# Three direct tiles in place of four per SwiGLU block, and the first round's additions to x by transfers from GpSimd

## The chip, the cores and the metric

The kernel runs on one core of one Trainium2 chip. The metric is the device time of one execution in microseconds (us); lower is better. The profile names the engines PE (TensorE, matmuls), PEld (its weight loads), DVE (VectorE), ACT (ScalarE), POOL (GpSimd) and SP (SyncE, which here issues transfers).

## The reference

One decoder layer of a Hymba/Conformer kind on 512 positions of width 1024, all in float32:

```python
x = x + 0.5 * swiglu(rms_norm(x, g_ffn1), w_ffn1_gate, w_ffn1_up, w_ffn1_down)
h = rms_norm(x, g_mix); proj = h @ w_in          # attention, conv and memory parts
...
x = x + concatenate([y_attn, y_conv, y_mem]) @ w_out
x = x + 0.5 * swiglu(rms_norm(x, g_ffn2), w_ffn2_gate, w_ffn2_up, w_ffn2_down)

def swiglu(x, w_gate, w_up, w_down):
    return (silu(x @ w_gate) * (x @ w_up)) @ w_down   # 1024 -> 2816 -> 1024
```

The change touches the two SwiGLU blocks alone; the mixing stage between them stays as it is.

## The kernel before

x lies in SBUF as eight tiles of 128 features by 512 positions (`x[:, d]`, d = 0 to 7). Every float32 product is made of three matmuls on split operands: each operand has a high part (`whi`, `xh`, `hh`, `bh`) and a low part (`wlo`, `xl`, `hl`, `bl`), and PE adds high by high, low by high and high by low in PSUM (`mm3`, L337 to L339).

**A SwiGLU block** (`ffn`) runs over 22 hidden tiles f of 128 features. The first `N_DIRECT` tiles are *direct*: gate and up take 24 matmuls of 512 columns each; `evac` (L403 to L410) scales the two products, applies the SiLU and multiplies, and `hidden` (L395 to L398) splits the result into `hh` (ACT) and `hl` (DVE). The remaining tiles are *fast* (`fast`): a scheme with fewer multiplications on two-by-two blocks makes gate and up out of seven half-size products (`product`, L439 to L441), 84 matmuls of 256 columns. It needs sums of blocks of x, which `blocks(k)` makes for k = 0 to 3 while the direct tiles run (`braw` and `bmade` on DVE, L427 to L429, their high parts `bh` on ACT, L426 and L430, their low parts `bl` on DVE, L431 and L432), and sums of the weights, `s12` and `s43`, which `make_sums` makes on DVE for each tile (L124 to L127). A few products pass through ACT (L450, L454, L456: PSUM to `kept`).

**Weights** (`Weights`) are loaded on SP's queue into four raw buffers (`wraw`), 512 KB at most each; ACT casts the high part (L165) and DVE subtracts for the low one (L166) into four slots used in turn. A slot is free when PE has read its last. In a name such as `wlo12` the number counts the weight pieces in order.

**The downs.** The hidden tiles are taken in rounds (`ROUNDS`). When a round is complete, `down(r, g)` multiplies its tiles with their part of the third weight, for each of the eight d, and DVE adds half the result to `x[:, d]` (L496). A load carries the weights of `8 // (tiles of the round)` of the d (`per_load`). `steps(f)` sets where they stand: the downs of a round lie among the tiles of the next one; those of the first round, all but the last load, stand ahead of the next round's first tile, which is the first fast one.

The order on each engine is fixed when the kernel is built, by a scheduler that moves instructions within what data and buffers allow; each engine then works its own list in order and waits at semaphores. Small work tiles `t` (`work()`) share five buffers in turn; PSUM has four banks for `mm`, two for `sc`, two for `tp`.

Of the kernel before, what the change touches and what calls it, by code (L numbers as in the profile page):

```python
# [34 lines left out]
AF = mybir.ActivationFunctionType  # L35
ALU = mybir.AluOpType
# [35 lines left out]
TILES = [s[1:] for s in ORDER if s[0] == "p"]  # L72

ON_DVE = [(0,), (1, 3), (1, 3), (2, 3), (1, 3), (1, 3)]
ROUNDS = [(0, 4), (4, 8), (8, 12), (12, 16), (16, 18), (18, 22)]
N_DIRECT = 4
N_ACT = 20

SUM_BUFS = 3
# [4 lines left out]
class Weights:  # L84
# [95 lines left out]
    def next(self):  # L180
        i = self.at
        self.at += 1
        self.split_to(i + 1 + self.conv_ahead)
        return self.split.pop(i)


def per_load(r):

    return 8 // (ROUNDS[r][1] - ROUNDS[r][0])


def steps(f):

    r = next(r for r, (lo, hi) in enumerate(ROUNDS) if lo <= f < hi)
    if r == 0:
        return [], [], []
    i, n, m = f - ROUNDS[r][0], ROUNDS[r][1] - ROUNDS[r][0], KT // per_load(r - 1)
    if r == 1:
        return [(r - 1, g) for g in range(m - 1)] if i == 0 else [], [(r - 1, m - 1)] if i == 1 else [], []
    mine = [(r - 1, g) for g in range(i * m // n, (i + 1) * m // n)]  # L200
    return [], mine[:1], mine[1:]


def layer(tc, ctx, a):
    nc = tc.nc
    PE, ACT, DVE, POOL = nc.tensor, nc.scalar, nc.vector, nc.gpsimd
# [8 lines left out]
    def nm(s):  # L215
        uid[0] += 1
        return f"{s}_{uid[0]}"

    def mm_bank():
        return psum.tile([P, T], F32, tag="mm", name=nm("mm"), bufs=4)  # L220

    def sc_bank():
        return psum.tile([P, T], F32, tag="sc", name=nm("sc"), bufs=2)
# [4 lines left out]
    def work():  # L228
        return tmp.tile([P, T], F32, tag="t", name=nm("t"), bufs=5)
# [7 lines left out]
    def flat(w):  # L237
        return w.rearrange("p k m -> p (k m)")

    def ffn_weights(n, memory):  # L240
        gu = a[f"wgu{n}"]

        def down(r, g):
            lo, hi = ROUNDS[r]
            m = per_load(r)
            return a[f"wd{n}"][g * m : (g + 1) * m, :, lo:hi].rearrange("d p k m -> p d (k m)")

        for f in range(NF):
            pre, mid, post = steps(f)
            for d in pre:  # L250
                W.add(down(*d), 128)
            if f < N_DIRECT:
                W.add(flat(gu[f, 0]))
# [5 lines left out]
            if memory and f == MEM_F:  # L259
                for t in range(2):  # L260
                    W.add(flat(a["wmk"][t]))
                for c in range(2):
                    W.add(flat(a["wmv"][:, 4 * c : 4 * c + 4]))
        r = len(ROUNDS) - 1
        for g in range(KT // per_load(r)):
# [21 lines left out]
    def atile(name, dtype=F32R):  # L287
        return act.tile([P, T], dtype, tag="h", name=nm(name), bufs=N_ACT)
# [45 lines left out]
    def mm3(ps, wh, wl, ks, hi, lo, first, last, woff=0):  # L334
        for i, k in enumerate(ks):
            w = slice((k - woff) * P, (k - woff + 1) * P)
            PE.matmul(ps, wh[:, w], hi(k), start=first and i == 0, stop=False)  # L337
            PE.matmul(ps, wh[:, w], lo(k), start=False, stop=False)  # L338
            PE.matmul(ps, wl[:, w], hi(k), start=False, stop=last and i == len(ks) - 1)  # L339
# [4 lines left out]
    def scaled_split(d, gcol):  # L344

        g = par[:, gcol + d : gcol + d + 1]
        xh[d], xl[d] = atile("xh"), atile("xl")
        ACT.activation(xh[d], x[:, d], AF.Identity, scale=g)
        DVE.scalar_tensor_tensor(xl[d], x[:, d], g, xh[d].bitcast(F32), op0=ALU.mult, op1=ALU.subtract)  # L349
# [39 lines left out]
    def ffn(pool, norm, first, gain, hooks, next_gain, last):  # L389
# [5 lines left out]
        def hidden(f, t):  # L395
            h_hi[f], h_lo[f] = atile("hh"), atile("hl")
            ACT.copy(h_hi[f], t)
            DVE.tensor_tensor(h_lo[f], t, h_hi[f].bitcast(F32), op=ALU.subtract)  # L398
# [13 lines left out]
        def blocks(k):  # L412

            raw = pool.tile([P, 4, 256], F32, tag="sum", name=nm("braw"), bufs=SUM_BUFS)
            made = pool.tile([P, 4, 256], F32, tag="sum", name=nm("bmade"), bufs=SUM_BUFS)
            flat_raw = raw.rearrange("p a b -> p (a b)")
            for i, d in enumerate((k + 4, k)):
                DVE.scalar_tensor_tensor(
                    flat_raw[:, i * T : (i + 1) * T], x[:, d], par[:, gain + d : gain + d + 1], rb, op0=ALU.mult, op1=ALU.mult
                )  # L420
            b21, b22, b11, b12 = (raw[:, i] for i in range(4))
            bh[k] = pool.tile([P, 7, 256], F32R, tag="bh", name=nm("bh"), bufs=4)
            bl[k] = pool.tile([P, 7, 256], F32R, tag="bl", name=nm("bl"), bufs=4)
            if k == 0:
                pool.tile([P, 16], F32, name=nm("shift"))
            ACT.copy(bh[k][:, 4:7], raw[:, 0:3])  # L426
            DVE.tensor_tensor(made[:, B_T3 : B_Q1 + 1], raw[:, 1:3], raw[:, 3:4].to_broadcast([P, 2, 256]), op=ALU.subtract)  # L427
            DVE.scalar_tensor_tensor(made[:, B_Q2], made[:, B_T3], -1.0, b11, op0=ALU.mult, op1=ALU.subtract)
            DVE.tensor_tensor(made[:, B_T4], b21, made[:, B_Q2], op=ALU.add)  # L429
            ACT.copy(bh[k][:, 0:4], made)  # L430
            DVE.tensor_tensor(bl[k][:, 4:7], raw[:, 0:3], bh[k][:, 4:7].bitcast(F32), op=ALU.subtract)  # L431
            DVE.tensor_tensor(bl[k][:, 0:4], made, bh[k][:, 0:4].bitcast(F32), op=ALU.subtract)  # L432
# [46 lines left out]
        def down(r, g):  # L479

            lo, hi = ROUNDS[r]
            end = r == len(ROUNDS) - 1
            wh, wl = W.next()

            def step(j):
                d = g * per_load(r) + j
                cut = last and end and d == KT - 1
                for t0, t1 in [(0, T // 2), (T // 2, T)] if cut else [(0, T)]:
                    ps = mm_bank()[:, : t1 - t0]
                    mm3(  # L490
                        ps, wh, wl, range(lo, hi), lambda k: h_hi[k][:, t0:t1], lambda k: h_lo[k][:, t0:t1],
                        True, True, woff=lo - j * (hi - lo),
                    )
                    xd = x[:, d, t0:t1]
                    o = work()[:, : t1 - t0] if last and end else xd
                    DVE.scalar_tensor_tensor(o, ps, 0.5, xd, op0=ALU.mult, op1=ALU.add)  # L496
                    if last and end:
                        nc.sync.dma_start(a["out"][d, :, t0:t1], o)
                if end and not last:
                    nxt.add(d)  # L500
                    scaled_split(d, next_gain)

            return [lambda j=j: step(j) for j in range(per_load(r))]
# [3 lines left out]
        raw = {}  # L507
        for f in range(NF):
            pre, mid, post = steps(f)
            for d in pre:  # L510
                for step in down(*d):
                    step()
            if f >= N_DIRECT:
                fast(f, mid)
            else:
                g, u = (sc_bank(), sc_bank()) if f % 3 == 2 else (mm_bank(), mm_bank())
                gh, gl = W.next()
                if f == 0:
                    uh, ul = W.next()
                    for ks in first:  # L520
                        mm3(g, gh, gl, ks, xhk, xlk, ks[0] == 0, ks[-1] == 7)
                        mm3(u, uh, ul, ks, xhk, xlk, ks[0] == 0, ks[-1] == 7)
                    norm.stats()
                    held = (g, u)
                else:
                    mm3(g, gh, gl, range(8), xhk, xlk, True, True)
                    if f == 1:
                        norm.spread()
                        raw[0] = evac(0, *held)
                        blocks(0)  # L530
                        hidden(0, raw[0])
                    uh, ul = W.next()
                    mm3(u, uh, ul, range(8), xhk, xlk, True, True)
                    raw[f] = evac(f, g, u)
                    if f == 1:
                        hidden(1, raw[1])
                    blocks(f)
                if f == N_DIRECT - 1:
                    for i in range(2, N_DIRECT):
                        hidden(i, raw[i])  # L540
            for d in post:
                for step in down(*d):
                    step()
            for hook in hooks.get(f, ()):
                hook()
        r = len(ROUNDS) - 1
# [168 lines left out]
    with tc.tile_pool(name="fast1", bufs=1) as pool:  # L715
        norm = ffn(pool, norm, STARTS, C_G1, hooks, C_GM, False)
# [4 lines left out]
    with tc.tile_pool(name="fast2", bufs=1) as pool:  # L721
        ffn(pool, norm, [[0, 1, 2, 3, 4, 5, 6], [7]], C_G2, {}, None, True)
# [484 lines left out]
```

## Time and profile before

| | |
|---|---|
| runs | 883.81, 884.22, 884.62 us; median 884.22 |
| the profiled execution | 884.99 us, span 883.2 us |
| first block: direct tile 4, downs of round 0, first fast tile | start at 48.01, 59.00, 75.80 us |
| second block: the same | start at 573.59, 584.58, 601.38 us |

The span is the time from the first to the last instruction that the profiler recorded; times in the trace count from its start. The profiled execution is one more run beside the three. The lines themselves are shown with the prediction.

### The profile page before, as it was taken

The page shows a single profiled execution, that of the slowest core. Times are in us where ns is not written, and L with a number is a line of the kernel's source. Part 1 is how long each engine was busy: PE and PEld are TensorE (multiplying, and loading weights), DVE is VectorE, ACT ScalarE, POOL GpSimd, SP SyncE. Part 2 cuts the span into 40 slices and gives each one's busy share as a digit, 9 for nine tenths or more (in the row PEclk, how much of TensorE's full clock was granted, in tenths as well). Part 3 has the DMA queues.
Part 4 walks back from the last instruction along what each step waited for, and adds up shares of the span by engine and source line. Part 5 has one row for each costly group of instructions (what it writes and reads, how often), then busy time and mean ns, then how long its engine had stood idle before and what let it go on. Part 6 is the DMA issues. An engine that isn't in the chain of part 4 may idle for free.

```text
span 883.2 us, 13993 instructions
## 1 busy us (share of the span) xinstructions
PE 869.9 (98%) x5522; PEld 760.4 (86%) x5525; DVE 713.1 (81%) x1121; ACT 438.2 (50%) x733; POOL 45.9 (5%) x38
## 2 busy tenths in 40 slices
PE   7999999999999999999999999999999999999998
PEld 3889999899999999888666788889999999989997
DVE  7999978986796886769999776999987878777872
ACT  6454554454563445533929754345554444534540
POOL 6000000000020000300020021000000000000000
PEclk9999999999999999999999999999999999999999
DMA  5522333333334244231010232323334332332312
GB/s 196 167 96 86 106 120 108 109 108 119 119 121 129 87 120 144 72 101 60 4 57 13 84 100 92 96 72 124 104 107 120 96 118 85 111 117 72 120 48 96
DMA packets 34082, 88.45 MB, mean 100 GB/s; under 512 B 3168, under 2 KB 7008, under 8 KB 34016
## 3 DMA queue, kind: packets, MB, share of 16 engines
q1 hardware_dynamic: 32864, 85.99, 30.9%
q10 hardware_dynamic: 1152, 1.57, 0.6%
q8 instruction: 43, 0.70, 0.3%
q14 instruction: 23, 0.19, 0.1%
HBM read 85.45 MB, written 2.10 MB: 99 GB/s over the span
## 4 chain that ended last, share of the span: by engine, by line
PE 93%; DVE 4%; DMA 1%; issue 1%; ACT 0%; SPq 0%; DVEq 0%
PE mm L337 15%; PE mm L339 15%; PE mm L338 15%; PE mm L439 11%; PE mm L441 11%; PE mm L440 11%; PE sc L439 2%; PE sc L441 2%; PE sc L440 2%; PE sc L337 1%; PE sc L339 1%; PE sc L338 1%; PE tp L924 1%; PE sc L863 1%; DVE conv L788 1%
## 5 line engine op out<-in xcount | busy, mean ns | idle before, releaser
L439 PE MATMUL mm<-bh,whi 128*128 128x256 f32 x864 | 239.8, 278 | 0.7 <-ACT kept L450 0.4
L441 PE MATMUL mm<-bh,wlo 128*128 128x256 f32 x864 | 239.2, 277 | 0.0
L440 PE MATMUL mm<-bl,whi 128*128 128x256 f32 x864 | 239.2, 277 | 0.0
L165 ACT CAST whi<-wraw 128x1024 fp32r<-128x1024 f32 (+2 forms) x122 | 124.3, 1021 | 125.2 <-PE mm L338 54.2
L166 DVE TENSOR_TENSOR wlo<-wraw,whi 128x1024 fp32r<-128x1024 f32 (+2 forms) x122 | 144.8, 1189 | 31.6 <-ACT whi L165 31.3
L439 PEld LDWEIGHTS mm<-bh,whi 128*128 128x128 f32 x864 | 162.3, 188 | 2.2 <-ACT kept L450 0.6
L440 PEld LDWEIGHTS mm<-bl,whi 128*128 128x128 f32 x864 | 162.7, 188 | 1.2
L441 PEld LDWEIGHTS mm<-bh,wlo 128*128 128x128 f32 x864 | 162.2, 188 | 0.0
L339 PE MATMUL mm<-hh,wlo 128*128 128x512 f32 (+1 forms) x356 | 139.4, 393 | 0.0
L338 PE MATMUL mm<-hl,whi 128*128 128x512 f32 (+1 forms) x356 | 139.4, 393 | 0.0
L337 PE MATMUL mm<-hh,whi 128*128 128x512 f32 (+1 forms) x356 | 138.6, 392 | 0.0
L166 DVE TENSOR_TENSOR wlo<-s,whi 128x1024 fp32r<-128x1024 f32 x72 | 88.4, 1229 | 28.7 <-ACT whi L165 28.5
L165 ACT CAST whi<-s 128x1024 fp32r<-128x1024 f32 x72 | 75.5, 1050 | 52.7 <-PE mm L440 36.5
L339 PEld LDWEIGHTS mm<-hh,wlo 128*128 128x128 f32 x356 | 66.9, 188 | 15.4
L339 PE MATMUL mm<-xh,wlo 128*128 128x512 f32 x192 | 76.4, 398 | 2.8 <-DVE wlo L178 2.8
L337 PEld LDWEIGHTS mm<-hh,whi 128*128 128x128 f32 x356 | 66.9, 188 | 13.5
L338 PEld LDWEIGHTS mm<-hl,whi 128*128 128x128 f32 x356 | 67.0, 188 | 13.4
L338 PE MATMUL mm<-xl,whi 128*128 128x512 f32 x192 | 75.9, 395 | 1.9 <-DVE xl L349 1.7
L337 PE MATMUL mm<-xh,whi 128*128 128x512 f32 x192 | 76.6, 401 | 0.6 <-ACT whi L177 0.6
L496 DVE SCALAR_TENSOR_TENSOR x<-mm,x 128x512 f32<-128x512 f32 x88 | 59.5, 684 | 9.9 <-PE mm L339 9.7
L460 ACT ACTIVATE t<-t 128x512 f32<-128x512 f32 x36 | 22.8, 632 | 56.2 <-DVE t L459 56.2
L165 ACT CAST vhi<-wraw 128x512 fp32r<-128x512 f32 x36 | 22.3, 621 | 52.6 <-PE sc L440 38.2
(245 smaller groups left out, 1395.7 us busy)
## 6 DMA issues: line engine op xcount, KB each, us to landing
wraw<-in_wgu SPq DMA_DIRECT2D x86, 512.0 KB, 3.5
wraw<-in_wd SPq DMA_DIRECT2D x44, 512.0 KB, 3.6
wraw<-in_win SPq DMA_DIRECT2D x12, 512.0 KB, 3.5
out<-t SPq DMA_DIRECT2D x7, 256.0 KB, 2.0
x<-in_xT SPq DMA_DIRECT2D x3, 512.0 KB, 5.9
wraw<-in_wout_a SPq DMA_DIRECT2D x6, 256.0 KB, 2.6
t<-in_memT ACTq DMA_DIRECT2D x4, 256.0 KB, 3.2
wraw<-in_wmk SPq DMA_DIRECT2D x2, 512.0 KB, 4.0
```

Source lines behind the costliest of these rows:

```text
L165: nc.scalar.copy(hi[:, :cols], raw[:, :cols])
L166: nc.vector.tensor_tensor(lo[:, :cols], raw[:, :cols], hi[:, :cols].bitcast(F32), op=ALU.subtract)
L337: PE.matmul(ps, wh[:, w], hi(k), start=first and i == 0, stop=False)
L338: PE.matmul(ps, wh[:, w], lo(k), start=False, stop=False)
L339: PE.matmul(ps, wl[:, w], hi(k), start=False, stop=last and i == len(ks) - 1)
L439: PE.matmul(ps, wh[:, c], bh[k][:, block], start=one, stop=False, skip_group_check=not first)
L440: PE.matmul(ps, wh[:, c], bl[k][:, block], start=False, stop=False, skip_group_check=not first)
L441: PE.matmul(ps, wl[:, c], bh[k][:, block], start=False, stop=end, skip_group_check=not first)
L460: ACT.activation(g, g, AF.Silu)
L496: DVE.scalar_tensor_tensor(o, ps, 0.5, xd, op0=ALU.mult, op1=ALU.add)
L788: DVE.scalar_tensor_tensor(conv[:, i], pad[:, i, j : j + T], w(i, j), conv[:, i], op0=ALU.mult, op1=ALU.add)
L863: PE.matmul(banks[h][:, i * ML + c.start : i * ML + c.stop], self.q[rows, n * P : (n + 1) * P], self.kt[rows, ks], start=not self.win, sto ...
```

## The change

Three direct tiles in place of four; the rounds become 3, 4, 4, 4, 4, 3 in place of 4, 4, 4, 4, 2, 4. The downs of the first round no longer add to x on DVE: ACT writes half the product from PSUM into a work tile (L497 of the changed kernel), and a transfer from POOL's queue adds that tile, 256 KB, to `x[:, d]` (L498), eight times a block. `hidden` follows each direct tile's evacuation at once, and `blocks(3)` follows `blocks(2)` in the third tile.

```diff
 TILES = [s[1:] for s in ORDER if s[0] == "p"]
 
 ON_DVE = [(0,), (1, 3), (1, 3), (2, 3), (1, 3), (1, 3)]
-ROUNDS = [(0, 4), (4, 8), (8, 12), (12, 16), (16, 18), (18, 22)]
-N_DIRECT = 4
+ROUNDS = [(0, 3), (3, 7), (7, 11), (11, 15), (15, 19), (19, 22)]
+N_DIRECT = 3
 N_ACT = 20
 
 SUM_BUFS = 3
@@ -492,6 +492,11 @@
                         True, True, woff=lo - j * (hi - lo),
                     )
                     xd = x[:, d, t0:t1]
+                    if r == 0:
+                        o = work()
+                        ACT.activation(o, ps, AF.Copy, scale=0.5)
+                        POOL.dma_start(xd, o, accum_op=ALU.add)
+                        continue
                     o = work()[:, : t1 - t0] if last and end else xd
                     DVE.scalar_tensor_tensor(o, ps, 0.5, xd, op0=ALU.mult, op1=ALU.add)
                     if last and end:
@@ -532,12 +537,10 @@
                     uh, ul = W.next()
                     mm3(u, uh, ul, range(8), xhk, xlk, True, True)
                     raw[f] = evac(f, g, u)
-                    if f == 1:
-                        hidden(1, raw[1])
+                    hidden(f, raw[f])
                     blocks(f)
-                if f == N_DIRECT - 1:
-                    for i in range(2, N_DIRECT):
-                        hidden(i, raw[i])
+                    if f == 2:
+                        blocks(3)
             for d in post:
                 for step in down(*d):
                     step()
```

A round of three has `per_load` 2, so a block has 24 loads for its downs in place of 22, of the same bytes together.

How the engines' lists change about the first fast tile. In a name such as `mm_81_693<-bh_41_349,whi12_626` the tile written stands first, then what is read; the last number of each only counts tiles. PE, first block, before: the first fast tile's second accumulator (`mm_81`), from the second weight piece to the third, which is made from the weight sum.

```order
L439 MATMUL mm_81_693<-bh_68_569,whi11_586 128x256
L440 MATMUL mm_81_693<-bl_69_570,whi11_586 128x256
L441 MATMUL mm_81_693<-bh_68_569,wlo11_587 128x256
L439 MATMUL mm_81_693<-bh_41_349,whi12_626 128x256 [waits Activation_49]
L440 MATMUL mm_81_693<-bl_42_350,whi12_626 128x256
L441 MATMUL mm_81_693<-bh_41_349,wlo12_627 128x256
L439 MATMUL mm_81_693<-bh_52_407,whi12_626 128x256
L440 MATMUL mm_81_693<-bl_53_408,whi12_626 128x256
```

PE, first block, after: the same place, with `wlo10` in the part of `wlo12`.

```order
L441 MATMUL mm_81_615<-bh_66_505,wlo9_515 128x256
L439 MATMUL sc_82_616<-bh_41_349,vhi12_621 128x256
L440 MATMUL sc_82_616<-bl_42_350,vhi12_621 128x256
L439 MATMUL mm_89_743<-bh_41_349,whi13_650 128x256 [waits Activation_49]
L440 MATMUL mm_89_743<-bl_42_350,whi13_650 128x256
L439 MATMUL mm_90_744<-bh_41_349,whi13_650 128x256 [waits Activation_49]
L440 MATMUL mm_90_744<-bl_42_350,whi13_650 128x256
L439 MATMUL mm_81_615<-bh_41_349,whi10_552 128x256 [waits Activation_49]
L440 MATMUL mm_81_615<-bl_42_350,whi10_552 128x256
L439 MATMUL mm_80_614<-bh_41_349,whi10_552 128x256
L440 MATMUL mm_80_614<-bl_42_350,whi10_552 128x256
L441 MATMUL mm_81_615<-bh_41_349,wlo10_553 128x256 [waits DVE_49]
```

Ten matmuls that use neither half of the weight sum's low part (of `sc_82`, `mm_89`, `mm_90` and of `whi10` itself) now stand ahead of the matmul that waits for `wlo10`; with the 24 above them of `mm_80` and `mm_81` they are 34 from the tile's start. In the second block the list has 46 there. Its end, with `wlo144` in the part of `wlo10`:

```order
L441 MATMUL sc_659_6083<-bh_643_5972,vlo146_6089 128x256
L439 MATMUL mm_666_6210<-bh_618_5816,whi147_6117 128x256
L440 MATMUL mm_666_6210<-bl_619_5817,whi147_6117 128x256
L439 MATMUL mm_667_6211<-bh_618_5816,whi147_6117 128x256
L440 MATMUL mm_667_6211<-bl_619_5817,whi147_6117 128x256
L439 MATMUL sc_668_6212<-bh_618_5816,vhi151_6248 128x256 [waits Activation_49]
L440 MATMUL sc_668_6212<-bl_619_5817,vhi151_6248 128x256
L441 MATMUL mm_658_6082<-bh_618_5816,wlo144_6020 128x256 [waits DVE_49]
L439 MATMUL mm_658_6082<-bh_629_5874,whi144_6019 128x256
```

ACT, first block, before: from the last block of x (`bh_68`) to the first copy out of the first fast tile (`kept_83`).

```order
L430 CAST bh_68_569<-bmade_67_566 128x1024 [waits DVE_49]
L165 CAST whi12_626<-s12_11_620 128x1024 [waits DVE_49,PE_49,Activation_49]
L165 CAST whi13_660<-s43_11_621 128x1024 [waits DVE_49,PE_49,Activation_49]
L165 CAST whi15_728<-wraw13_533 128x1024 [waits DMAHW4_49,PE_49,Activation_49]
L450 COPY kept_83_695<-mm_80_692 128x256 [waits PE_49]
L454 ACTIVATE kept_84_696<-mm_81_693 128x256 [waits PE_49,Activation_49]
```

ACT, first block, after:

```order
L497 ACTIVATE t_77_598<-mm_76_588 128x512 [waits PE_49,Activation_49]
L165 CAST whi13_650<-wraw11_452 128x1024 [waits DMAHW2_49,PE_49]
L497 ACTIVATE t_79_611<-mm_78_601 128x512 [waits DMASW0_49,PE_49,Activation_49]
L450 COPY kept_83_617<-mm_80_614 128x256 [waits PE_49]
L430 CAST bh_66_505<-bmade_65_502 128x1024 [waits DVE_49]
L165 CAST whi10_552<-s12_9_546 128x1024 [waits DVE_49]
L165 CAST whi11_584<-s43_9_547 128x1024 [waits DVE_49]
L454 ACTIVATE kept_84_618<-mm_81_615 128x256 [waits PE_49]
```

The cast of the last block of x (`bh_66` now) and that of the weight sum (`whi10`) have come to stand behind the last copies of the first round, the cast `whi13` and the first copy of the fast tile. `t_79` waits for a semaphore of POOL's transfers (DMASW), since it takes the buffer that `t_69` had.

DVE, first block, before: from the last block of x to the weight sum's low part.

```order
L432 TENSOR_TENSOR bl_69_570<-bmade_67_566,bh_68_569 128x1024 [waits Activation_49]
L496 SCALAR_TENSOR_TENSOR x_69<-mm_74_592,x_69 128x512 [waits PE_49]
L496 SCALAR_TENSOR_TENSOR x_69<-mm_75_606,x_69 128x512 [waits PE_49]
L124 TENSOR_TENSOR s12_11_620<-wraw12_503 128x512 [waits DMAHW3_49]
L127 TENSOR_TENSOR s43_11_621<-wraw11_452,wraw12_503 128x512
L125 TENSOR_TENSOR s12_11_620<-wraw11_452,s12_11_620 128x512 [waits DVE_49]
L496 SCALAR_TENSOR_TENSOR x_69<-mm_76_632,x_69 128x512 [waits PE_49]
L126 TENSOR_TENSOR s43_11_621<-wraw11_452,s12_11_620 128x512 [waits DVE_49]
L166 TENSOR_TENSOR wlo12_627<-s12_11_620,whi12_626 128x1024 [waits Activation_49]
```

DVE, first block, after:

```order
L124 TENSOR_TENSOR s12_9_546<-wraw10_422 128x512 [waits DMAHW1_49]
L429 TENSOR_TENSOR bmade_65_502<-braw_64_501,bmade_65_502 128x256 [waits DVE_49]
L125 TENSOR_TENSOR s12_9_546<-wraw9_367,s12_9_546 128x512 [waits DVE_49]
L127 TENSOR_TENSOR s43_9_547<-wraw9_367,wraw10_422 128x512 [waits DVE_49]
L432 TENSOR_TENSOR bl_67_506<-bmade_65_502,bh_66_505 128x1024 [waits Activation_49]
L126 TENSOR_TENSOR s43_9_547<-wraw9_367,s12_9_546 128x512 [waits DVE_49]
L166 TENSOR_TENSOR wlo10_553<-s12_9_546,whi10_552 128x1024 [waits PE_49,Activation_49]
```

The three additions to x between them are gone, and the weight sum's operations stand around the last block's.

## The prediction

> **What bounds the kernel now.** I read the busy shares first, then the chain that ended last, then the waits of PE, and last the two places that the change touches.
>
> ```profile
> PE 869.9 (98%) x5522; PEld 760.4 (86%) x5525; DVE 713.1 (81%) x1121; ACT 438.2 (50%) x733; POOL 45.9 (5%) x38
> PEclk9999999999999999999999999999999999999999
> PE 93%; DVE 4%; DMA 1%; issue 1%; ACT 0%; SPq 0%; DVEq 0%
> PE mm L339 <- DVE wlo L178: 2.8, 4, 0.9
> PE mm L439 <- ACT kept L450: 0.4, 1, 0.4
> PE mm L439 <- ACT kept L454: 0.3, 1, 0.3
> ```
>
> The first row is busy time by engine, the second the clock that PE was granted, the third the chain, the others some of PE's waits (total, times, longest). PE is busy for 98% of the span at full clock and carries 93% of the chain. The largest of its waits comes to 2.8 us in all, so time can be won by giving PE less to do, and lost only where another engine becomes late for PE. DVE is at 81% and can become late; ACT at 50% has room on the average, but works in order.
>
> The stretches that matter, in both SwiGLU blocks: the fourth direct tile, the downs of the first round, and the first fast tile.
>
> ```profile
> 48.01:59.00 10.99, 10.99 (x49) 9.02 (x48) 10.89 (x16) 6.42 (x8) 0.00 (x0) 1.00 0.34 104
> 59.00:75.80 16.80, 16.80 (x73) 13.54 (x72) 16.74 (x24) 6.17 (x8) 0.00 (x0) 1.00 0.19 61
> 75.80:85.32 9.52, 9.52 (x85) 9.52 (x84) 8.48 (x11) 5.50 (x9) 0.00 (x0) 1.00 0.37 112
> 573.59:584.58 10.99, 10.99 (x49) 9.02 (x48) 10.81 (x17) 6.80 (x9) 0.00 (x0) 1.00 0.41 127
> 584.58:601.38 16.80, 16.80 (x73) 13.54 (x72) 16.26 (x23) 5.70 (x7) 0.00 (x0) 1.00 0.14 43
> 601.38:610.90 9.52, 9.52 (x85) 9.52 (x84) 8.69 (x12) 5.24 (x9) 0.00 (x0) 1.00 0.34 110
> ```
>
> Columns: length, then busy time and instructions of PE, its weight loads, DVE, ACT and POOL, then clock, DMA share and GB/s. PE has no gap in any of them. DVE is full in the direct tile and in the downs, and POOL does nothing.
>
> **The change, part by part.**
>
> *One direct tile becomes a fast one, in each block.* 10.99 goes, 9.52 comes: −1.47 a block, **−2.94** in all, on PE's own path. The matmuls of the downs stay the same in number; with three tiles in the first round and three in the last, a few go from one place to another at 16.80 / 72 = 0.233 us each. The four further loads carry the same bytes on a queue that leaves the DMA engines two thirds idle here (0.34 and 0.41): nothing.
>
> *The first fast tile comes nearer to what feeds it.* Let T be its start. Ahead of it, PE loses the direct tile and a quarter of the round's downs (18 of 72 matmuls, 4.20): T falls from 75.80 to 60.61, and from 601.38 to 586.19. That is 15.2 us less cover for DVE and ACT, which make the weight sums, the splits and the last block of x.
>
> ```profile
> 62.88 0.95 DVE L431 TENSOR_TENSOR bl<-braw,bh 128x768 fp32r<-128x768 f32 x1
> 63.75 0.42 DVE L428 SCALAR_TENSOR_TENSOR bmade<-bmade,braw 128x256 f32<-128x256 f32 x1
> 66.76 1.22 DVE L432 TENSOR_TENSOR bl<-bmade,bh 128x1024 fp32r<-128x1024 f32 x1
> 67.90 1.28 DVE L496 SCALAR_TENSOR_TENSOR x<-mm,x 128x512 f32<-128x512 f32 x2
> 69.09 0.68 DVE L124 TENSOR_TENSOR s<-wraw 128x512 f32<-128x512 f32 x1
> 69.69 0.69 DVE L127 TENSOR_TENSOR s<-wraw,wraw 128x512 f32<-128x512 f32 x1
> 72.18 1.23 DVE L166 TENSOR_TENSOR wlo<-s,whi 128x1024 fp32r<-128x1024 f32 x1
> 597.28 1.22 DVE L166 TENSOR_TENSOR wlo<-s,whi 128x1024 fp32r<-128x1024 f32 x1
> ```
>
> DVE, start and duration. From start to start an operation takes 0.60 (512 columns), 0.87 (768) or 1.14 (1024). The low half of the first weight sum (wlo12 before, wlo10 after) started at 72.18, 3.6 us ahead of T. After the change DVE is rid, ahead of it, of three operations of an evacuation (1.81), two splits of 1024 (2.28), 0.27 in each of three splits that become 768 wide (0.81), a low half of a hidden tile (0.60) and three additions to x (1.80): 7.30. DVE by itself would start it at 64.88 = T + 4.27 in the first block, and 7.30 earlier at 589.98 = T + 3.79 in the second. So it is behind T already by DVE's work alone, and ACT is a little later still:
>
> ```profile
> 49.26 1.05 ACT L430 CAST bh<-bmade 128x1024 fp32r<-128x1024 f32 x1 [0.19 <-DVE bmade L429]
> 50.22 0.63 ACT L406 ACTIVATE t<-t 128x512 f32<-128x512 f32 x1
> 54.47 0.83 ACT L426 CAST bh<-braw 128x768 fp32r<-128x768 f32 x1
> 55.21 0.61 ACT L397 CAST hh<-kept 128x512 fp32r<-128x512 f32 x1
> 75.81 1.05 ACT L165 CAST whi<-wraw 128x1024 fp32r<-128x1024 f32 x1 [2.46 <-PE mm L338]
> 77.37 0.37 ACT L450 COPY kept<-mm 128x256 f32<-128x256 f32 x1 [0.51 <-PE mm L441]
> 81.45 0.37 ACT L456 COPY kept<-mm 128x256 f32<-128x256 f32 x1
> 81.72 1.05 ACT L165 CAST whi<-s 128x1024 fp32r<-128x1024 f32 x1
> L927 ACT COPY pt<-tp 128x512 f32<-128x512 f32 x16 | 9.2, 594 | 3.3 <-PE tp L924 3.1
> ```
>
> The order on ACT after the change is: the cast whi13, the last of the first round's copies (t_79, L497), L450, the cast of the last block of x (bh_66, L430), whi10. The cast whi13 waits until PE has left its slot, at the last down matmul; its like did that at 75.81 = T + 0.01. A cast of 1024 gives way after 0.96 (49.26 to 50.22): t_79 starts at T + 0.97. It takes about 0.60 (the like copy from PSUM has 0.594). L450 follows at T + 1.57, which is also when PE's first product is ready (77.37 − 75.80). After 0.27 (81.45 to 81.72) bh_66 starts, at T + 1.84, and ends at T + 2.89. DVE waits for it with L432, behind which stand L126 and wlo10: T + 2.93, 1.14, 0.60, so wlo10 starts at T + 4.67 and ends 1.22 later, at **T + 5.89**. whi10 is cast from T + 2.80 to T + 3.85.
>
> PE's side: the order puts work that needs neither half ahead of that wait, 34 matmuls in the first block, 46 in the second, at 9.52 / 84 = 0.1133: 3.85 and 5.21 us. In the first block PE comes to whi10 after 30 (T + 3.40, waits 0.45) and then to wlo10 and waits 1.59: 2.04. In the second it waits 5.89 − 5.21 = 0.68. Together **+2.72**. Such a wait is paid in full, as PE has no slack behind it. The following pieces are in time again: wlo11 is the next split but one on DVE (T + 7.6 against a need at T + 8.4).
>
> *The additions to x by transfers.* DVE is rid of eight operations a block; apart from the three counted above, PE never waited for them: nothing. ACT gets eight copies of 0.60 a block, 4.8 in some 17 us in which it was busy for 6.17: room, except at the place just counted. POOL's transfers are new:
>
> ```profile
> out<-t SPq DMA_DIRECT2D x7, 256.0 KB, 2.0
> t<-in_memT ACTq DMA_DIRECT2D x4, 256.0 KB, 3.2
> x<-in_xT SPq DMA_DIRECT2D x3, 512.0 KB, 5.9
> ```
>
> Issues: KB, median us to landing. No row shows an accumulating transfer. t_79 goes into the buffer of the first copy, t_69, and so waits for that transfer to land. On ACT t_69 stands behind the cast of bh_62 and hh_58, which come out of the third tile's evacuation; that tile ended at 48.01, and I count on the same end after the change. Before, the like pair (54.47 and 55.21 above) gave way to the next cast by 55.8; I put the issue of t_69 at 55.4, since fewer casts stand ahead of it. t_79 is wanted at T + 0.97 = 61.58, a window of 6.2 us (5.8 in the second block, the same count there). The bounds are 2.0 from below and 5.9 + 1.75 (POOL's longest operation, quoted below, for making the descriptors) = 7.65 from above. I take 3.2, a row of 256 KB that was read under load: it lands in time, price 0, keeping 0 to 7.65 − 6.2 + 7.65 − 5.8 = 3.3. POOL's issues also wait for earlier readers of x; behind them on POOL stands only the mixing stage's work, hundreds of us later.
>
> By the Trainium skill ("DMA: Bandwidth & Descriptors", section "Anatomy of one DMA — SWDGE (gpsimd) path") a GpSimd transfer takes some 2.0 us and its bytes at 436 GB/s, by which I estimate 2.6 us for 256 KB and a sum with no lateness; no run here has shown one so far.
>
> *Sum.* −2.94 + 2.72 = −0.22 on a profiled execution of 884.99 (span 883.2 and 1.8 around it), which lies 0.77 above the median of 884.22: 884.77 profiled, **884.0 against the median**. What can be told from no change is 0.2%, 1.77 us: this is none.
>
> **The rivals.**
>
> *PE's cover hides the wait: faster.* If the chain on ACT and DVE is 2 us shorter than I have it (the scheduler's order of a cast apart, or bh_66 done before T), the whole 2.94 stays: 881.3. For it: the waits of 0.4 and 0.3 behind L450 and L454 are all that PE's fast tiles lose to ACT now. Against it: DVE alone cannot start wlo10 before T + 3.79 and end it before T + 5.0, which in the first block is 1.16 behind PE's 3.85.
>
> *The first transfer lands late: slower.* From 6.2 us on (5.8 in the second block) each further us holds up t_79, with it L450, bh_66, wlo10 and PE, one for one. At the upper bound that is 3.3 us: 887.3. This is the mechanism that ends on the other side, and it decides from about 1 us of lateness a block.
>
> *DVE and POOL get into each other's way: slower.*
>
> ```profile
> 354.85 1.75 POOL L366 TENSOR_TENSOR sqsum<-sqsum,t 128x512 f32<-128x512 f32 x1 [10.34 <-ACT t L362]
> 355.35 1.79 DVE L349 SCALAR_TENSOR_TENSOR xl<-x,par,xh 128x512 fp32r<-128x512 f32 x1
> 543.13 0.74 DVE L349 SCALAR_TENSOR_TENSOR xl<-x,par,xh 128x512 fp32r<-128x512 f32 x1
> ```
>
> The same DVE operation took 1.79 beside an operation of POOL and 0.74 without one: 1.05 more. If each issue of a transfer cost DVE as much, the six ahead of wlo10 would put it 6.3 us back in each block: 12.6, 896.6 at the most. Below, an issue reads no tile, and may cost 0; it could not win anything, as it only adds. I take 0, since the row is of an operation that reads and writes tiles.
>
> The Trainium skill ("SBUF — State Buffer", section "Who interferes with whom") has a rule that speaks against the change: a DVE operation with two SBUF inputs contends with a GpSimd operation that reads SBUF, and a transfer from GpSimd's queue stalls when its descriptors cannot be written because DVE is in a two-port mode. The pair of rows above agrees with its first half. By the rule itself the operations beside the issues, with two inputs at 0.60 per 512 columns, hold the read side alone, so the sum by it is the one above; in the other reading it is this rival's.
>
> **How the numbers follow.** No measurable change 0.47; cover holds (881.3) 0.17; transfer late (up to 887.3) 0.15; DVE and POOL (885 to 896.6) 0.15; something else 0.06, a third on each side. Faster: 0.17 + 0.02 = 0.19. Slower, past 885.99: 0.15 + 0.15 + 0.02 = 0.32. Same: 0.49. The predicted time is that of the likeliest, 884.0. The range takes in the faster case and the late transfer's bound and the lower part of the last rival: 881.2 to 888.5.
>
> **What would show it.** Right: PE waits of about 2.0 and 0.7 us for wlo10 and its like in the second block's first fast tile, the first fast tile 11.6 and 10.2 long instead of 9.52, starting near 60.6 and 586; the transfers land in 2 to 4 us. Wrong: no such wait (faster); or L497 of t_79 waiting for a DMA, or DVE operations of over 0.9 per 512 columns beside POOL's issues between 50 and 62 (slower). The weakest steps are PE's order, which puts 34 and 46 matmuls ahead of the wait, and the T + 1.84 of bh_66, which hangs on the order that ACT was given.

## The result and the profile after

The changed kernel takes 890.85 us (median of 8 runs, 885.88 to 894.57) against 884.45 (8 runs, 883.21 to 884.67): ratio 1.0075, 95% interval 1.0061 to 1.0089. It is slower by 6.4 us where no measurable change was forecast (884.0, range 881.2 to 888.5), and its runs spread over 8.7 us where those of before spread over 1.5. The profiled execution took 891.54.

In this section and the next a *fast matmul* is one of a fast tile (256 columns), whatever its pace, and a *down matmul* is one of the downs (512 columns).

The page of the changed kernel: busy shares, granted clock, chain, and the transfers.

```profile
PE 873.8 (98%) x5594; PEld 766.6 (86%) x5594; DVE 712.0 (80%) x1121; ACT 453.4 (51%) x765; POOL 60.5 (7%) x54
PEclk9999999999999999999999999999999999999999
PE 92%; DVE 5%; DMA 1%; ACT 1%; issue 1%; SPq 0%; DVEq 0%; ACTq 0%
x<-t POOLq DMA_DIRECT2D x16, 256.0 KB, 5.1
```

PE still has no room: 98%, at full clock. Its waits (total, times, longest) show the two that were forecast for the first block, none of their kind for the second, and one at the copies of a later tile that grew from 0.4 to 1.0:

```profile
PE mm L441 <- DVE wlo L166: 1.3, 1, 1.3
PE mm L439 <- ACT kept L450: 1.0, 1, 1.0
PE mm L439 <- ACT whi L165: 0.4, 1, 0.4
```

Waits are not the whole of it. Windows of the changed kernel, first over the first fast tile of each block, then over a later tile of 84 matmuls with its 24 down matmuls; and windows of the kernel before over the same kind of tile, one in the second block and one in the first (columns as in the prediction):

```profile
61.20:73.24 12.04, 10.30 (x85) 9.89 (x84) 12.04 (x18) 7.01 (x10) 1.15 (x2) 1.00 0.73 157
587.63:598.00 10.37, 10.23 (x85) 9.78 (x84) 10.27 (x15) 6.74 (x11) 0.86 (x1) 1.00 0.88 189
690.61:706.09 15.48, 15.48 (x110) 14.41 (x109) 11.70 (x16) 7.36 (x11) 0.00 (x0) 1.00 0.33 103
```

```profile
675.30:690.42 15.12, 15.12 (x109) 14.04 (x108) 11.88 (x16) 7.38 (x12) 0.00 (x0) 1.00 0.37 112
150.27:165.75 15.48, 15.48 (x109) 14.41 (x108) 15.34 (x25) 6.95 (x11) 0.00 (x0) 1.00 0.38 106
```

In the third row PE is busy all the time, at clock 1.00, waits for nothing, and still takes 15.48 for what took 15.12 before. The difference lies in the fast matmuls alone: a fast tile takes 9.90 or 9.52 us, 117.8 or 113.3 ns from the start of one matmul to the start of the next. There are two paces, and the last row shows that the kernel before knew the slow one too. Counted over the trace, it had 553 fast matmuls at the slow pace, the changed kernel has 1705. Of these 1455 are in the second block, all but five of them behind 607, where no fast matmul is at the other pace any more.

So the 6.55 us between the two profiled executions are: −2.94 for the two direct tiles, +2.51 and +0.84 for the first fast tiles (12.04 and 10.37 against 9.53), (1705 − 553) × 4.4 ns = +5.1 for the pace, and +0.6 for the copy's wait. Together 6.1. About 0.2 of the slow pace lies in the first fast tiles and is counted in both terms, so some 0.7 is not accounted for.

### The profile page after: what moved, and what is told of

It reads as the page before. It is cut to its first block, busy times and chain, and to the rows that moved or that the text cites. A ratio compares the mean times of both kernels' runs of the same rounds, so it can differ in the third digit from the quotient of the medians.

```text
span 889.8 us, 14254 instructions
## 1 busy us (share of the span) xinstructions
PE 873.8 (98%) x5594; PEld 766.6 (86%) x5594; DVE 712.0 (80%) x1121; ACT 453.4 (51%) x765; POOL 60.5 (7%) x54
## 3 DMA queue, kind: packets, MB, share of 16 engines
q10 hardware_dynamic: 1152, 1.57, 0.5%
## 4 chain that ended last, share of the span: by engine, by line
PE 92%; DVE 5%; DMA 1%; ACT 1%; issue 1%; SPq 0%; DVEq 0%; ACTq 0%
PE mm L337 14%; PE mm L339 14%; PE mm L338 14%; PE mm L441 12%; PE mm L439 11%; PE mm L440 11%; PE sc L439 2%; PE sc L440 2%; PE sc L441 2%; PE sc L339 1%; PE sc L337 1%; PE sc L338 1%; PE tp L927 1%; PE sc L866 1%; DVE conv L791 1%
## 5 line engine op out<-in xcount | busy, mean ns | idle before, releaser
L439 PE MATMUL mm<-bh,whi 128*128 128x256 f32 x912 | 254.6, 279 | 1.7 <-ACT kept L450 1.0
L441 PE MATMUL mm<-bh,wlo 128*128 128x256 f32 x912 | 253.4, 279 | 1.3 <-DVE wlo L166 1.3
L440 PE MATMUL mm<-bl,whi 128*128 128x256 f32 x912 | 253.9, 279 | 0.0
L439 PEld LDWEIGHTS mm<-bh,whi 128*128 128x128 f32 x912 | 171.4, 188 | 3.8 <-ACT kept L450 1.2
L440 PEld LDWEIGHTS mm<-bl,whi 128*128 128x128 f32 x912 | 173.0, 190 | 1.4
L441 PEld LDWEIGHTS mm<-bh,wlo 128*128 128x128 f32 x912 | 170.7, 188 | 1.7 <-DVE wlo L166 1.7
L339 PE MATMUL mm<-xh,wlo 128*128 128x512 f32 x160 | 63.7, 398 | 2.7 <-DVE wlo L178 2.7
L338 PE MATMUL mm<-xl,whi 128*128 128x512 f32 x160 | 63.5, 397 | 1.8 <-DVE xl L349 1.7
L337 PE MATMUL mm<-xh,whi 128*128 128x512 f32 x160 | 64.2, 403 | 1.0 <-ACT whi L177 0.9
L501 DVE SCALAR_TENSOR_TENSOR x<-mm,x 128x512 f32<-128x512 f32 x72 | 49.3, 686 | 16.5 <-PE mm L339 16.4
```

What stands on the lines that cost most here:

```text
L439: PE.matmul(ps, wh[:, c], bh[k][:, block], start=one, stop=False, skip_group_check=not first)
L440: PE.matmul(ps, wh[:, c], bl[k][:, block], start=False, stop=False, skip_group_check=not first)
L441: PE.matmul(ps, wl[:, c], bh[k][:, block], start=False, stop=end, skip_group_check=not first)
```

## What sets the pace

The starts in the trace show it, in nanoseconds. In a run of down matmuls their spacing alternates between 236 and 231. Where the last spacing ahead of a fast matmul is 236, the fast matmuls that follow are spaced by 113.3; where it is 231, by 117.8. The eleven traces of this study (both kernels and nine experiments) have 607 groups of down matmuls that stand between two fast matmuls and have no wait inside. 450 of them ended with 236, and the fast pace followed every time. 157 ended with 231 (about 226 where the group is a single down matmul), and the slow pace followed 154 times; in two of the other three the spacing does not alternate (233 and 234). As the spacing alternates, an even number of down matmuls keeps the pace and an odd number turns it:

| groups of downs between fast matmuls | fast to fast | fast to slow | slow to slow | slow to fast |
|---|---|---|---|---|
| even number | 429 | 0 | 132 | 8 |
| odd number | 1 | 18 | 4 | 15 |

(A few matmul records can be missing from a trace, so that single counts can be off.) The rule has exceptions. The eight even groups that went from slow to fast, and two of the four odd ones that stayed slow, stand behind a stretch of fast matmuls in which PE had waited (a step above 125 ns), and PE comes off a wait at either pace. The other two odd groups that stayed slow had no wait ahead of them: they are the second group of nine of the second block in the changed kernel, and the same group in the kernel with one matmul more below. Only there do 22 fast matmuls stand since the group before; in all other slow stretches without a wait there are 24, 60, 144 or 228. So the number of fast matmuls may count as well; no experiment tests this.

The kernel before has odd groups at one place alone, in its first block, where a group of 12 is split into 1 and 11 (246.9 and 249.9), slow between them. The change put odd groups into both blocks: a round of three tiles has 3 × 3 = 9 down matmuls for each d, and the two d of the first round's last load stand one by one in the second fast tile. In the second block the first group of nine turned the pace from fast to slow at 607, the other left it there, all later groups have 12, and PE never waits again: the slow pace lasts to the end of the block. The first fast tile behind the two groups:

```profile
611.82:621.72 9.90, 9.90 (x86) 9.90 (x85) 9.90 (x14) 6.33 (x11) 0.86 (x1) 1.00 0.64 155
```

Had the second group of nine turned the pace back, as it did in the first block (85.2), only the 22 matmuls between them would have been slow, 0.1 us. So that the whole block was slow hangs on the exception above as well as on the rule.

## The experiments

Theory A is this pace by odd and even; theory B, the rival, that the transfers from POOL disturb PE. Each kernel's ratio is to the kernel before, run beside it on the same chip; it is worked out from all runs of both, with a 95% interval in brackets. Behind a time the brackets hold the lowest and the highest run.

**The rounds alone.** The `if r == 0` branch is taken out of the changed kernel:

```diff
-                    if r == 0:
-                        o = work()
-                        ACT.activation(o, ps, AF.Copy, scale=0.5)
-                        POOL.dma_start(xd, o, accum_op=ALU.add)
-                        continue
```

> The changed kernel with the first round's additions to x back on DVE; three direct tiles and the new rounds stay, the transfers from POOL are gone. Theory A (pace): PE's fast matmuls run at one of two paces, 113.3 or 117.8 ns, and a group with an odd number of down matmuls between them (the nine of a round of three tiles) can switch it. The two groups of nine are still here, so the second block again runs most of its 19 fast tiles at 9.90 us: 888 to 893. Theory B (the transfers are what costs, by their load on DVE, ACT or the memory): with them gone the kernel comes back to 884 or below, tiles at 9.53.

895.38 us, ratio 1.0136 (1.0111 to 1.0161). Without the transfers the kernel is slower still, so B falls. The second block runs at the slow pace (1560 matmuls of it, 32 at the fast one), as A said, but the time is above A's 888 to 893, because PE now waits for DVE's additions to free its accumulators (total, times, longest, in a profiled run of 900.59, the slowest of the six):

```profile
PE mm L337 <- DVE x L496: 8.0, 3, 5.2
PE mm L439 <- DVE x L496: 1.5, 1, 1.5
```

**The transfers alone.** The same branch is put into the kernel before.

> The kernel before with the other half of the change alone: the first round's additions to x by transfers from POOL; four direct tiles and the old rounds stay, so every group of down matmuls between fast ones has an even number. Theory A (pace by odd groups): no lasting slow pace beyond what the kernel before shows (374 and 179 slow matmuls in its two blocks, 2.5 us), the first fast tiles start behind 72 down matmuls and wait little: 883.5 to 885.5. Theory B (the transfers disturb PE): 888 to 892, with slow tiles in the second block.

885.73 (884.42 to 888.90), ratio 1.0008 (0.9995 to 1.0020): no difference that can be told, and 0.2 above A's range. The profile is of the run of 888.90; even so its second block has 31 slow matmuls. The transfers do not bring the slow pace.

**One matmul more in the kernel before.**

```diff
+                    if last and (r, d) in [(1, 2)]:
+                        PE.matmul(ps, wh[:, j * (hi - lo) * P : (j * (hi - lo) + 1) * P], h_hi[lo][:, t0:t1], start=True, stop=True)
                     mm3(
```

> The kernel before with one matmul more (128x128 by 512 columns, 0.23 us): in the second block the first matmul of the third d of round 1 is done twice, which makes one group of 12 down matmuls a group of 13. Theory A (pace): from there on, from about 652 to 855, the second block's fast tiles run at 9.90 in place of 9.53: 13 tiles by 0.37 and 0.2 for the matmul, 884.3 + 5 = 889. Theory B (the two paces come from something else, load on SBUF or the memory): 884.5, the price of the matmul.

888.40 (887.90 to 889.63), ratio 1.0047 (1.0030 to 1.0064). One matmul of 0.23 us, whose result the next one overwrites, costs 4.3 (888.40 against 884.09), near A's 889. Windows ahead of the group of 13 and behind it:

```profile
644.60:659.72 15.12, 15.12 (x111) 14.04 (x110) 12.38 (x19) 7.84 (x13) 0.00 (x0) 1.00 0.37 106
690.65:706.13 15.48, 15.48 (x110) 14.41 (x109) 11.70 (x17) 7.37 (x11) 0.00 (x0) 1.00 0.34 116
```

**Two matmuls more there**, a group of 14: the added line stands twice.

> The kernel before with the first matmul of the third d of round 1 of the second block done three times: a group of 14, even, where the kernel with one more matmul had 13 and took 888.4. Theory A (odd and even): the fast pace stays through that group, 884.4 + 2 x 0.23 = 884.9, though there is more work than with 13. If any disturbance of the groups of 12 led to the slow pace: 888.7.

885.20 (883.76 to 885.90), ratio 1.0008 (0.9999 to 1.0017). Twice the added work, and 0.75 above its kernel before, where one matmul cost 4.3. The same window stays at the fast pace:

```profile
690.62:705.74 15.12, 15.12 (x109) 14.04 (x108) 10.63 (x16) 6.93 (x11) 0.00 (x0) 1.00 0.33 94
```

**Two odd groups, two rounds apart**, with `[(1, 2), (3, 2)]` in the condition.

> As the kernel with one group of 13, and the first matmul of the third d of round 3 is done twice as well, some 5 to 6 tiles on. Theory A (pace as a matter of odd and even): the second odd group can put PE back to the fast pace, so only the tiles between the two run at 9.90: 884.3 + 0.5 + 6 x 0.37 = 887. If an odd group only ever leads to the slow pace: 889.3. Theory B: 884.8.

887.64 (885.89 to 891.27), ratio 1.0041 (1.0024 to 1.0059). The profile has the slow pace from the first odd group (669) to the second (789) and the fast one after it. The second group was one of 37, since three loads stand together there; some seven and a half tiles lie between (624 slow matmuls in the block), not six.

**One matmul more in the changed kernel**, with `[(1, 0)]`, behind the two groups of nine.

> The changed kernel with one down matmul more (0.23 us): in the second block the first matmul of the first d of round 1 is done twice, a group of 13 behind the two groups of nine. Theory A (an odd group takes PE from the slow pace back to the fast one, too): where the second block was slow from 607 on, it is fast again from about 640 on, 16 tiles by 0.37: 5.9 less, 885 to 886; in a run whose second block was fast there, it would now be slow. Theory B (the pace does not hang on the count): 891, the matmul's price more.

887.05 (885.92 to 892.08), ratio 1.0036 (1.0019 to 1.0053), where the changed kernel stands at 1.0075. More work, less time, though 1 us more than A's 885 to 886. Two of its ten runs, 891.70 and 892.08, are as slow as the changed kernel; they have no traces. The profile is of a run of 888.46. Ahead of the group of 13 is a stretch of fast matmuls alone, 10.00 us, with starts 117.8 ns apart (x87 counts those cut at its edges, too); behind the group is a tile of 84 with its 24 down matmuls, at the fast pace:

```profile
628.00:638.00 10.00, 10.00 (x87) 10.00 (x87) 9.10 (x13) 6.20 (x11) 0.00 (x0) 1.00 0.32 107
648.97:664.09 15.12, 15.12 (x110) 14.04 (x108) 10.68 (x16) 6.94 (x11) 0.00 (x0) 1.00 0.30 91
```

**The two groups of nine as one of 18.**

```diff
             if rest:
                 rest.pop(0)()
+            if f == N_DIRECT + 1:
+                rest.pop(0)()
```

> The changed kernel with one move: the two d of the first round's last load run one behind the other in the second fast tile, 18 down matmuls in one group in place of 9 and 9. The same work, the same transfers. Theory A (pace by odd groups): the second block stays at the pace that it has after its first fast tile, which was 113.3 ns, to its end; 6.3 us come back there, 884.5 to 886; where the waits in the first fast tile of a block leave PE at the slow pace, that pace now stays (up to 3 us more in the first block, 6.5 in the second). Theory B (transfers): no change, 889 to 892.

887.29 (884.70 to 894.01), ratio 1.0044 (1.0024 to 1.0063): 3.2 us above its kernel before, where the change lost 6.4; the expected 884.5 to 886 is missed. Nine of twelve runs lie under 888.3 and three at 890.9 to 894.0. The profile is of one of the latter (892.85) and shows why: the group of 18 kept the fast pace, and 8 us later a wait of under 0.1 us ended it.

```profile
618.60 0.28 PE L441 MATMUL mm<-bh,wlo 128*128 128x256 f32 x1
618.71 0.34 PE L439 MATMUL mm<-bh,whi 128*128 128x256 f32 x1
618.89 0.28 PE L440 MATMUL mm<-bl,whi 128*128 128x256 f32 x1
619.00 0.28 PE L441 MATMUL mm<-bh,wlo 128*128 128x256 f32 x1
```

The step from 618.71 to 618.89 is 0.18 in place of 0.11. At that place ACT is at a fast tile's copies: one (L454) ended at 618.61, and the weight load of the matmul of 618.71 began 0.05 behind it. From there the pace is slow to the end of the block (15.48 a tile). The kernel before has the same in its first block: a step of 0.16 at 124.93, and the slow pace from there to 172.7. So a short wait is a second way into the slow pace; that it explains the spread of the changed kernel's runs too is likely, but those runs have no traces.

**All four loads of the first round ahead of the first fast tile**, in the changed kernel:

```diff
     if r == 1:
-        return [(r - 1, g) for g in range(m - 1)] if i == 0 else [], [(r - 1, m - 1)] if i == 1 else [], []
+        return [(r - 1, g) for g in range(m)] if i == 0 else [], [], []
```

> The changed kernel with all four loads of the first round ahead of the first fast tile: 72 down matmuls there, and none of the groups of nine between fast tiles. The same work. Theory A (pace by odd groups, and a first fast tile that comes too early): the second block runs at 9.53 a tile, and the first fast tiles are covered by 4.2 us more work of PE, so their waits (2.5 and 0.85) go in part: 881 to 884, faster than the kernel before by up to 2.9. Theory B (transfers): 888 to 891, or slower as they come closer together.

881.70 (880.86 to 881.87), ratio 0.9957 (0.9943 to 0.9972): faster than both kernels, and its runs lie within 1.0 us. There are no groups of nine between fast tiles, and the first fast tiles, with 4.2 us more of PE's work ahead of them, find everything ready:

```profile
65.69:75.21 9.52, 9.52 (x85) 9.52 (x84) 9.49 (x12) 6.78 (x12) 0.86 (x1) 1.00 0.93 216
588.62:598.14 9.52, 9.52 (x85) 9.52 (x84) 9.48 (x12) 6.78 (x12) 0.86 (x1) 1.00 0.91 212
```

**The same without the transfers.**

> All four loads of the first round ahead of the first fast tile, as in the kernel that took 881.7, but the additions to x on DVE and no transfers from POOL. What the transfers are worth once the pace is out of the way. If DVE is late without them, as PE's 8 us of waits for x with the rounds alone say: 886 to 892, with the waits in the downs of the first round. If the transfers only move work: 881 to 882.

889.60 (888.41 to 890.87), ratio 1.0060 (1.0047 to 1.0072): 7.9 us more than with them, and the pace is fast in the second block (34 slow matmuls). PE waits for DVE's additions:

```profile
PE mm L337 <- DVE x L496: 5.1, 4, 1.6
PE mm L439 <- DVE x L496: 1.4, 2, 0.7
```

With three direct tiles the transfers are what lets the first round's downs run without a wait. Neither half of the change wins alone; together, with the downs in one piece, they win 2.9 by the medians (3.8 by the ratio). That this is also the 2.94 of the two tiles is in part chance: the profile of the kernel that takes 881.70 has 177 slow matmuls, 376 fewer than that of the kernel before (1.7 us), and some 0.7 us more of waits at the copies of later tiles.

## Why the prediction was wrong, step by step

*The tile's price, where it failed.* The step "10.99 goes, 9.52 comes" held at the fast pace. What failed is the step that a fast tile has one price, 9.52, wherever it stands, and that down matmuls moved "from one place to another" cost 0.233 each and nothing else. The runs showed in its place that a fast tile costs 9.52 or 9.90 by what stands ahead of it: 1152 more fast matmuls at the slow pace, +5.1 us, for which the sum had nothing. I read the price from the first fast tiles and not from the others; the row 150.27 to 165.75 above, 15.48 against 15.12, was in the trace of before. The pace was no rival of mine. The measured time lies among those of my last rival, DVE and POOL (885 to 896.6), but only by chance, as DVE's rows below show.

*The first fast tile: right, a little too small.* T was 61.20 for 60.61 and 587.63 for 586.19. ACT and DVE did in the first block what the order said (start, duration):

```profile
61.16 1.05 ACT L165 CAST whi<-wraw 128x1024 fp32r<-128x1024 f32 x1 [0.83 <-PE mm L338]
62.12 0.58 ACT L497 ACTIVATE t<-mm 128x512 f32<-128x512 f32 x1
62.77 0.37 ACT L450 COPY kept<-mm 128x256 f32<-128x256 f32 x1
63.15 1.05 ACT L430 CAST bh<-bmade 128x1024 fp32r<-128x1024 f32 x1
64.23 1.22 DVE L432 TENSOR_TENSOR bl<-bmade,bh 128x1024 fp32r<-128x1024 f32 x1
65.98 1.22 DVE L166 TENSOR_TENSOR wlo<-s,whi 128x1024 fp32r<-128x1024 f32 x1
```

wlo10 started at T + 4.78, forecast T + 4.67. The waits of 0.4 and 1.3 were forecast as 0.45 and 1.59; from start to start of the matmuls they took 0.6 and 1.5. Behind each of them one more step took 0.22 in place of 0.11, and 51 matmuls at the slow pace come on top: the tile lost 2.51 against 2.04. In the second block wlo144 started at 592.30, T + 4.67 as forecast, but the loss of 0.84 is not the one wait of 0.68 for it. PE lost 0.3 ahead of that, at the matmul of sc_668 that waits for a cast on ACT (vhi151), which I had not counted, 0.15 for wlo144, and the rest in steps behind the waits. Together +3.35 in place of +2.72. (That DVE alone ends wlo10 1.16 behind PE's 3.85 mixes the two blocks; with the first block's T + 4.27 it is 1.64. The argument stands.)

*The transfers.* They took 5.1 us (3.3 to 7.0 from issue to landing), not 3.2. t_79 had no wait for its buffer even so: the row at 62.12 starts where whi13's 0.96 end. The Trainium skill's figure ("DMA: Bandwidth & Descriptors", section "Anatomy of one DMA — SWDGE (gpsimd) path"), from which I had estimated 2.6, is half of what these accumulating transfers took here. The price of 0 held, since the transfers that count, the first of each block, took 4.1 and 3.4: t_69's was issued at 56.25 and landed at 60.3, 1.8 us ahead of t_79, in place of the 3 that I had counted. With the longest, 7.0, it would have been late.

*DVE beside POOL: no price.* An issue keeps POOL busy for 0.87 us in the median, up to 1.5 where four follow one another, and the DVE operations beside the first four, from 56.25 to 59.94, take what they take alone (the last row):

```profile
56.25 3.69 POOL L498 DMA_DIRECT2D x<-t  x4 [35.14 <-DVE bmade L428]
56.10 0.75 DVE L418 SCALAR_TENSOR_TENSOR braw<-x,par,rb 128x512 f32<-128x512 f32 x1
57.10 0.75 DVE L418 SCALAR_TENSOR_TENSOR braw<-x,par,rb 128x512 f32<-128x512 f32 x1
43.85 0.75 DVE L418 SCALAR_TENSOR_TENSOR braw<-x,par,rb 128x512 f32<-128x512 f32 x1
```

The reading that I took of the Trainium skill's rule ("SBUF — State Buffer", section "Who interferes with whom"), that a DVE operation with two inputs contends only with an operation of POOL that reads tiles, agrees with these rows.

*DVE's relief.* "Apart from the three counted above, PE never waited for them: nothing" held against the kernel before, and hid what the transfers do: with three direct tiles PE would wait for the additions, 9.5 us by the first experiment's waits and 6.5 by the last one's.

*Open.* Why odd and even decide is not known: the runs show the rule, not the circuit behind it. Nor is it known why the second group of nine left the second block slow. What leaves PE at one pace or the other after a wait was not tried apart.

## What to carry to other kernels

Where PE is the bound, time one and the same piece of work at several places of the trace before giving it a price; a busy PE at full clock can run at more than one pace. When matmuls of another size are put between back-to-back ones, look at whether their number is odd, and at whether a short wait stands at the seam: here one matmul of 0.23 us cost 4.3, and two cost 0.8. Two halves of a change can each be worth nothing and win together, so try the order of the work before giving one up.

## What was not expected of the hardware

Matmuls of 128x128 by 256 columns with a new weight load each run at 113.3 or 117.8 ns, and can keep the pace for over 200 us (607 to 861 in the changed kernel). And behind some waits of PE the granted clock fell to half for 3.5 us: in the kernel with one matmul more, after the wait of 1.3 us for wlo10 in the first fast tile (first row the wait, second the dip, third after it), though the changed kernel has the same wait at the same place and no dip.

```profile
64.89:68.46 3.57, 1.83 (x13) 1.42 (x12) 3.57 (x5) 1.70 (x2) 0.00 (x0) 1.00 0.75 137
68.46:72.00 3.54, 3.54 (x20) 3.54 (x18) 3.54 (x5) 0.72 (x2) 0.00 (x0) 0.52 0.69 220
72.00:82.24 10.24, 10.24 (x89) 10.24 (x88) 8.94 (x12) 6.99 (x12) 0.00 (x0) 1.00 0.40 122
```

It costs about 1.5 us there (3.54 for 18 weight loads, which take 18 × 0.113 = 2.04 at full clock). The same came about fast tiles in two other kernels: behind a wait of 2.0 us in the one with the transfers alone, and at one of 5.2 in the one with the rounds alone, there for 6.8 us from within the wait. A wait of 1.6 in the kernel with one group of 18 brought none. Nor is it bound to such waits: the traces of all nine experiments have a dip of 3.4 or 6.8 us in their first 21 us, and those of the kernels before and after have none.
